# Moving operands of gate and up kept in DRAM as single values and split in place when loaded, the first pair of gate and up interleaved, and the first buffers of the way down moved

## The chip, the cores and the metric

The kernel runs on one core of a Trainium2 chip. The metric is the device time of one execution in microseconds (us). TensorE (PE) does the matrix products, VectorE (DVE) and ScalarE (ACT) the elementwise work, GpSimd (POOL) some elementwise work and the DMAs of one queue, SyncE (SP) issues the DMAs of the other.

## The reference, cut to what matters

One layer of a hybrid decoder: 2048 prompt tokens and 8 sample tokens, D_MODEL = 1024, D_FF = 2816.

```python
# n = RMSNorm(x); one projection of n, split among attention heads and gated linear attention (GLA)
# A = sliding-window attention with sinks, B = chunked GLA
# h = x + W_o [A | B]
# y = h + SwiGLU(RMSNorm(h)):  (silu(z @ w_gate) * (z @ w_up)) @ w_down,  z = RMSNorm(h)
```

All products are wanted to float32 accuracy.

## The kernel before, in words

The program runs through five stages, one after the other: attention (0 to about 380 us of the span), GLA (to 739), W_o with the second RMSNorm (to about 950), gate and up (959 to 1847), down (1853 to 2307). The order on each engine is fixed at build time by a scheduler that lists the instructions by a timeline of its own; engines run their lists in order and wait for each other by semaphores. Buffers lie in pools stacked in SBUF, so a pool of a later stage lies over buffers of an earlier one, and its first write waits for their last use.

**Split values.** A float32 operand is split into a high part (ACT, `split`, L92: a cast to the reduced type) and a low part (DVE or POOL, L93: value minus high part). A product is three matmuls (`mm3`, L104 to L106): high x high, high x low, low x high.

**W_o stage.** Token tiles of 128 run in the order 0, 4, 1, 5, 2, 6, 3, 7, then 8, 12, 9, ... , 15, then the decode tile (8 sample tokens, `ti == NB`). For each, `load_tile` loads the mixed heads (`mr`) and splits them into `mt`; `product` multiplies by W_o (`WO`, two halves of D, L104 to L106; the decode tile's product is L1019), adds h, and writes h to DRAM (L1022); `normalise` makes z (L1030 to L1032), transposes it (L1037, `ps_zT`) and puts it into four tiles `b`. When two tiles j = 0, 1 of one `mt` are there, `operands` forms the seven moving operands of Strassen's method (P1 to P7) from the quarters `b` by four subtractions `t`, **splits each one** into `zhl` (a ring of three buffers in the pool `hlp`) and writes high and low part to DRAM (`zc_d`, L1057, on POOL's queue). The last `mt` is 132 wide, since it takes the decode tokens with it, so its operands wait for the decode tile. `PRODS` is the order P1, P6, P2, P7, P5, P4, P3.

**Gate and up.** The tokens fall into two halves, sb = 0 (512 columns) and sb = 1 (516). At the start of a half the seven split operands `z` are loaded from `zc_d` on SP's queue (L1242, 2 MB each). Then 11 pairs of feed-forward blocks (`fp`) run. For each the weights of gate and of up are loaded (`wrg`, L1179) and turned into seven units each (`units`, `whl`, a ring of 7 buffers, which `dm` of the next stage shares): a sum or difference (L958, L961) and a split. A unit times its z is a product of 4 x 3 matmuls of 512 columns (2 x 12 of 258 at sb = 1). `Strassen.ready` takes the results from PSUM: P1 by ACT (L1149, `gp` for gate and `up` for up), the others by DVE; silu is ACT (L1191), the multiplication L1199. The combined results are written for the way down (`md_d`, L1236, POOL's queue), and the decode columns are kept in `mdec` by ACT (L1227).

**Down.** Four groups of pairs (3, 3, 3 and 2). A group loads W_down (`wrd`), makes seven split units per pair (`dhl`, 22 buffers), and for each of 8 token tiles loads `mr` from `md_d` (L1310), splits its seven parts into `dm`, and multiplies; `decode` does the sample tokens with `mhl`, the split of `mdec`. In SBUF the two `mr` buffers lie over the last z operands used (those of P4 and P3), the first `dhl` buffers over the z of P1, which is free earliest.

## Time and profile before

| | before |
|---|---|
| median of 3 runs | 2312.25 us (2310.04 to 2315.82) |
| profiled execution, and its span | 2311.51 us, 2309.7 us |
| mean granted clock of TensorE | 0.983 |
| PE busy | 2227.1 us, 96% of the span |
| DVE busy | 1600.5 us, 69% |
| ACT busy | 957.2 us, 41% |
| POOL busy | 623.8 us, 27% |
| moved by DMA | 364.57 MB, 158 GB/s on average |

The times of rows below are in us from the span's start; the profiled execution takes 1.8 us more than its span. A row of a timeline gives start, duration, engine (SPq is SP's DMA queue), line, operation, out<-in, and in brackets the idle time before it and what ended that. In a row of windows stand the length, the busy time of PE, PEld (weight loads), DVE, ACT and POOL with their instruction counts, the granted TensorE clock, the DMA share and GB/s. Matmuls are pipelined: what counts is the distance between two starts, not the duration shown.

### The profile page before, as it was taken

To read this page: it belongs to the slowest core of one execution; us is meant where nothing else is said; L and a number is where in the kernel's file an instruction comes from. 1 tells how busy PE (TensorE), PEld (TensorE's weight loads), DVE (VectorE), ACT (ScalarE), POOL (GpSimd) and SP (SyncE) were. 2 spreads that over 40 slices of the span, in tenths; PEclk is the share of its full clock that TensorE was granted. 3 is DMA by queue.
4 is the path that set the end of the run, shared out by engine and by line. 5 is a ranking of instruction groups with operands and counts; after the bars stand their busy time and mean duration, and the time that the engine had idled before them with its cause. 6 is when DMAs were issued, how large, how long until landed. Compare 5 with 4: busy or idle time off the path is not lost.

```text
span 2309.7 us, 34809 instructions
## 1 busy us (share of the span) xinstructions
PE 2227.1 (96%) x12649; PEld 1923.6 (83%) x12649; DVE 1600.5 (69%) x3236; ACT 957.2 (41%) x2120; POOL 623.8 (27%) x791
## 2 busy tenths in 40 slices
PE   8999998999999999699999999999999989999998
PEld 6888886788887788578888889999999968787887
DVE  6787887587776567556666666767676674847477
ACT  5676777343443234323232333333333243535342
POOL 2443434365465133201111110101010122222222
PEclk9999998999998999899999999999999999999999
DMA  7323234245325689872324257323233277878877
GB/s 239 122 75 115 93 108 153 90 157 165 126 87 214 225 275 288 276 247 87 119 79 127 78 177 290 110 84 115 87 111 97 83 225 171 210 165 213 185 184 263
DMA packets 204935, 364.57 MB, mean 158 GB/s; under 512 B 15411, under 2 KB 128332, under 8 KB 200780
## 3 DMA queue, kind: packets, MB, share of 16 engines
q1 hardware_dynamic: 167740, 258.80, 34.2%
q0 software_dynamic: 37024, 103.55, 17.9%
q8 instruction: 100, 1.64, 0.3%
q14 instruction: 71, 0.58, 0.1%
HBM read 211.09 MB, written 152.27 MB: 157 GB/s over the span
## 4 chain that ended last, share of the span: by engine, by line
PE 31%; issue 20%; POOL 5%; DMA 1%; DVE 0%; POOLq 0%; ACT 0%; SPq 0%; DVEq 0%; ACTq 0%
PE ps_b L105 4%; PE ps_b L104 4%; PE ps_b L106 4%; POOL h_d L1329 4%; PE ps_c L105 3%; PE ps_c L104 3%; PE ps_c L106 3%; PE ps_a L105 3%; PE ps_a L106 3%; PE ps_a L104 3%; POOL out_y_prompt_dram L1324 1%; DMA z<-zc_d_P 1%; POOL md_d L1236 1%; DMA zc_d_P<-zhl 0%; DMA wrg<-in_w_gate_dram 0%
## 5 line engine op out<-in xcount | busy, mean ns | idle before, releaser
L104 PE MATMUL ps_b<-z,whl 128*128 128x258 f32 (+1 forms) x792 | 253.8, 321 | 3.2 <-DMA z<-zc_d_P 3.2
L105 PE MATMUL ps_b<-z,whl 128*128 128x258 f32 (+1 forms) x792 | 254.0, 321 | 0.0
L106 PE MATMUL ps_b<-z,whl 128*128 128x258 f32 (+1 forms) x792 | 252.8, 319 | 0.0
L92 ACT CAST dm<-mr 128x384 fp32r<-128x384 f32 (+1 forms) x224 | 108.0, 488 | 188.4 <-PE ps_b L106 97.6
L104 PE MATMUL ps_a<-z,whl 128*128 128x258 f32 (+1 forms) x528 | 170.9, 324 | 8.3 <-DMA z<-zc_d_P 8.3
L105 PE MATMUL ps_a<-z,whl 128*128 128x258 f32 (+1 forms) x528 | 170.7, 323 | 0.0
L106 PE MATMUL ps_a<-z,whl 128*128 128x258 f32 (+1 forms) x528 | 170.3, 323 | 0.0
L104 PE MATMUL ps_c<-z,whl 128*128 128x258 f32 (+1 forms) x528 | 168.6, 319 | 0.9 <-DMA z<-zc_d_P 0.9
L105 PE MATMUL ps_c<-z,whl 128*128 128x258 f32 (+1 forms) x528 | 169.1, 320 | 0.0
L106 PE MATMUL ps_c<-z,whl 128*128 128x258 f32 (+1 forms) x528 | 168.9, 320 | 0.0
L104 PEld LDWEIGHTS ps_b<-z,whl 128*128 128x128 f32 x792 | 149.3, 189 | 15.9 <-DMA z<-zc_d_P 3.5
L106 PEld LDWEIGHTS ps_b<-z,whl 128*128 128x128 f32 x792 | 149.2, 188 | 12.1
L105 PEld LDWEIGHTS ps_b<-z,whl 128*128 128x128 f32 x792 | 149.2, 188 | 11.9
L93 DVE TENSOR_TENSOR dm<-mr,dm 128x384 fp32r<-128x384 f32 (+1 forms) x224 | 114.9, 519 | 59.4 <-ACT dm L92 59.4
L92 ACT CAST whl<-wrg 128x512 fp32r<-128x512 f32 x132 | 81.6, 620 | 150.5 <-PE ps_b L106 81.2
L802 POOL TENSOR_TENSOR bd<-E,qTb 64x128 f32<-64x128 f32 x224 | 127.1, 567 | 60.6 <-ACT E L787 47.2
L93 DVE TENSOR_TENSOR whl<-wrg,whl 128x512 fp32r<-128x512 f32 x132 | 90.9, 688 | 42.9 <-ACT whl L92 42.7
L961 DVE TENSOR_TENSOR gu<-ps_c,gu 128x512 f32<-128x512 f32 (+1 forms) x130 | 77.9, 600 | 61.0 <-PE ps_c L106 60.3
L1236 POOL DMA_DIRECT2D md_d<-m x22 | 15.7, 713 | 373.7 <-DVE m L1199 360.3
L104 PEld LDWEIGHTS ps_a<-z,whl 128*128 128x128 f32 x528 | 100.8, 191 | 17.0 <-issue 4.4
L104 PEld LDWEIGHTS ps_c<-z,whl 128*128 128x128 f32 x528 | 99.8, 189 | 9.3 <-ACT whl L92 1.3
L105 PEld LDWEIGHTS ps_a<-z,whl 128*128 128x128 f32 x528 | 100.5, 190 | 8.2
(385 smaller groups left out, 6625.9 us busy)
## 6 DMA issues: line engine op xcount, KB each, us to landing
mr<-md_d SPq DMA_DIRECT2D x24, 1344.0 KB
zc_d_P<-zhl POOLq DMA_DIRECT2D x49, 512.0 KB, 6.1
wrg<-in_w_gate_dram SPq DMA_DIRECT2D x44, 512.0 KB
wrg<-in_w_up_dram SPq DMA_DIRECT2D x44, 512.0 KB
nT_d<-nT SPq DMA_DIRECT2D x16, 1024.0 KB
zT<-nT_d SPq DMA_DIRECT2D x8, 2048.0 KB
z<-zc_d_P SPq DMA_DIRECT2D x7, 2064.0 KB
z<-zc_d_P SPq DMA_DIRECT2D x7, 2048.0 KB
```

Of the source, the lines that this page charges most:

```text
L92: nc.scalar.copy(h, src)
L93: (eng or nc.vector).tensor_tensor(l, src, h.bitcast(F32), ALU.subtract)
L104: nc.tensor.matmul(ps, lh, rh, start=start, stop=False, skip_group_check=more)
L105: nc.tensor.matmul(ps, lh, rl, start=False, stop=False, skip_group_check=more)
L106: nc.tensor.matmul(ps, ll, rh, start=False, stop=stop, skip_group_check=more)
L802: nc.gpsimd.tensor_tensor(bv[rows, :, h], eo, qo, ALU.mult)
L961: nc.vector.tensor_tensor(out, a, b, ALU.add)
L1236: nc.gpsimd.dma_start(md_d[sb][g][:, :, q, fp - GROUPS[g][0], :], src.rearrange("p (m t) -> p m t", m=4))
L1324: nc.gpsimd.dma_start(O["y_prompt"][0, ti * P:(ti + 1) * P, cols], hq[which])
L1329: nc.gpsimd.dma_start(h_d[ti][:, cols], c, accum_op=ALU.add)
```

## The change

Six edits go together.

- `zc_d` holds single values: `operands` writes `b` and `t` themselves, without the split and the ring `zhl`, half the bytes.
- Each z lies in a pool of its own. It is loaded into the low half of its tile and split there (`split_z`): the high part by ACT, two casts of 128 x 1024, the low part over the loaded value by DVE (P1, P2, P7) or POOL (P6, P5, P4, P3), two subtractions of 128 x 1024 each.
- The pools of W_o are cut so that the z of P1 lies over the two `mt` buffers alone, those of P6 and P2 over the first half of W_o and those of P7 and P5 over the second. The first two `mr` of that stage get buffers of their own. The write of the decode tile's h goes to POOL's queue.
- In the first pair of sb = 0 gate and up alternate in a fixed order, the splits of z are put behind named instructions (`issue_after`), P2's behind gate's copy of P1, and the weights of later pairs are loaded after the last z.
- The copies into `mdec` go from ACT to POOL.
- Down: the two `mr` buffers lie over the z of P1 and P6, the first six `dhl` over P6 and P2, the others below. In the first group pair 0's units come first, then those of pairs 1 and 2 in turn, and the low parts of pairs 0 and 2 are made by POOL.

```diff
-    zc_d = [[dram.tile([P, 2, KD // 2, WIDTHS[sb]], F32, name=f"zc_d{sb}_{q}") for q in PRODS] for sb in range(2)]
+    zc_d = [[dram.tile([P, KD // 2, WIDTHS[sb]], F32, name=f"zc_d{sb}_{q}") for q in PRODS] for sb in range(2)]
...
-        wop = pool(ph, "m_wo", 1, side="right")
-        hlp = pool(ph, "m_hl", 3, side="right")
+        wop = [pool(ph, f"m_wo{dh}", 1, side="right") for dh in range(2)]
+        mrp = pool(ph, "m_mr", 2, side="right")
...
-                mr = hlp.tile([P, 1056], F32, tag="hl", name="mr")[:, :1024]
+                mr = mrp.tile([P, 1024], F32, tag="mr", name="mr")
...
-            nc.sync.dma_start(h_d[ti] if ti < NB else hdec_d, h[:n])
+            (nc.sync if ti < NB else nc.gpsimd).dma_start(h_d[ti] if ti < NB else hdec_d, h[:n])
...
             for q, src in enumerate((b11, t2, b21, t3, t1, t4, b22)):
-                hl = hlp.tile([P, 2, 4, 132], F32R, tag="hl", name="zhl")
-                split(hl[:, 0, :, :w], hl[:, 1, :, :w], src)
-                nc.gpsimd.dma_start(zc_d[sb][q][:, :, :, mt * P:mt * P + w], hl[:, :, :, :w].bitcast(F32))
+                nc.gpsimd.dma_start(zc_d[sb][q][:, :, mt * P:mt * P + w], src)
...
-        zcp = pool(ph, "g_zc", 1, side="right")
+        zcp = {name: pool(ph, f"g_z{q}", 1, side="right") for q, name in enumerate(PRODS)}
...
-        def pair(sb, fp, zc):
+        def split_z(z, name, behind=()):
+            with ExitStack() as es:
+                for ins in behind:
+                    es.enter_context(tc.issue_after(ins.ins))
+                for ks in (slice(0, 2), slice(2, 4)):
+                    split(z[:, 0, ks], z[:, 1, ks], z[:, 1, ks].bitcast(F32), None if name in ("P1", "P2", "P7") else nc.gpsimd)
+        def pair(sb, fp, zc, ug, uu):
...
-            ug, uu = load_w(w_g, fp), load_w(w_u, fp)
+                return mm.ins
             if len(pieces) == 1:
+                last = None
                 for q in PRODS:
-                    prod(sg, q, next(ug))
-                    prod(su, q, next(uu))
+                    for st, us in ((sg, ug), (su, uu)):
+                        with tc.issue_after(last) if fp == 0 and last else nullcontext():
+                            with tc.issue_after(begun.pop().ins) if begun and fp == 1 else nullcontext():
+                                hl = next(us)
+                            last = prod(st, q, hl)
+                        if fp == 0:
+                            for name, *behind in {("P1", sg): (("P2", sg.kept),), ("P1", su): (("P7", su.kept),),
+                                                 ("P2", sg): (("P5", sg.silu),), ("P7", su): (("P4", sg.silu, su.mark),),
+                                                 ("P5", sg): (("P3", sg.silu),)}.get((q, st), ()):
+                                split_z(zc[name], name, behind)
+                if fp == 0:
+                    begun.extend([su.mark] * 4)
...
-                    nc.scalar.copy(mdec[:, 2 * fp + f, 4 * j:4 * j + 4], m[:, 512:516])
+                    nc.gpsimd.tensor_copy(mdec[:, 2 * fp + f, 4 * j:4 * j + 4], m[:, 512:516])
...
-            zc = {name: zcp.tile([P, 2, 4, 516], F32R, tag=f"z{q}", name=f"z{q}")[:, :, :, :WIDTHS[sb]]
-                  for q, name in reversed(list(enumerate(PRODS)))}
+            zc = {name: zcp[name].tile([P, 2, 4, 516], F32R, tag=f"z{q}", name=f"z{q}")[:, :, :, :WIDTHS[sb]]
+                  for q, name in enumerate(PRODS)}
+            raws = load_w(w_g, 0), load_w(w_u, 0)
             for q, name in enumerate(PRODS):
-                nc.sync.dma_start(zc[name].bitcast(F32), zc_d[sb][q])
+                come = nc.sync.dma_start(zc[name][:, 1].bitcast(F32), zc_d[sb][q])
+            for name in PRODS[:2] if sb == 0 else PRODS:
+                split_z(zc[name], name)
             for fp in range(NP):
-                pair(sb, fp, zc)
+                pair(sb, fp, zc, *raws)
+                if fp + 1 < NP:
+                    with tc.issue_after(come.ins):
+                        raws = load_w(w_g, fp + 1), load_w(w_u, fp + 1)
...
-        wdp = pool(ph, "d_w", 22, side="right")
-        mrp = pool(ph, "d_mr", 2, side="right")
+        mrps = [pool(ph, f"d_mr{i}", 1, side="right") for i in range(2)]
+        wdps = [pool(ph, f"d_w{i}", n, side="right") for i, n in enumerate((6, 8, 8))]
+        made = [0]
+        def unit_tile():
+            j = made[0] % 22
+            made[0] += 1
+            return wdps[(j >= 6) + (j >= 14)].tile([P, 2, 512], F32R, tag="w", name="dhl")
...
-                uq = {}
-                b = (r0[:, 0:512], r0[:, 512:], r1[:, 0:512], r1[:, 512:])
-                for q, src in zip(PRODS, sums_b(*b)):
-                    hl = wdp.tile([P, 2, 512], F32R, tag="w", name="dhl")
-                    split(hl[:, 0], hl[:, 1], src)
-                    uq[q] = hl
-                us.append(uq)
+                for q, src in zip(PRODS, sums_b(r0[:, 0:512], r0[:, 512:], r1[:, 0:512], r1[:, 512:])):
+                    hl = unit_tile()
+                    split(hl[:, 0], hl[:, 1], src, nc.gpsimd if p in (0, 2) else None)
+                    us[p - p0][q] = hl
+                    yield
+            for some in ([[p0], [p0 + 1, p0 + 2]] if g == 0 else [[p] for p in range(p0, p1)]):
+                for _ in zip(*[pair_units(p) for p in some]):
...
-                mr = mrp.tile([P, 7, 384], F32, tag="mr", name="mr")[:, :, :npr * P]
+                mr = mrps[mi % 2].tile([P, 7, 384], F32, tag="mr", name="mr")[:, :, :npr * P]
```

`issue_after(x)` makes the scheduler list what stands under it behind x; it adds no wait on the chip.

On SP's queue the first load of z (P1's) now stands ahead of the last prompt tile's write of h, and no write of the decode tile's h stands in front of the others; before, all seven stood behind it. On PE, at the end of W_o, before (z_10184 is P1's z):

```order
L1019 MATMUL ps_wo<-WO_8479,mixdec 40x512 x16
L1019 MATMUL ps_wo<-WO_8480,mixdec 40x512 x16
L1037 MATMUL ps_zT<-ident,z 128x128 x8
L1037 MATMUL ps_zT<-ident,z 128x8 x8
L104 MATMUL ps_a<-z_10184,whl 128x512
```

Now the transposes of the decode tile (`128x8`) stand behind the products P1 and P6 of gate and of up, 48 matmuls later (z_10033 is P6's z, z_10034 P2's):

```order
L105 MATMUL ps_b<-z_10033,whl 128x512
L106 MATMUL ps_b<-z_10033,whl 128x512
L1038 MATMUL ps_zT<-ident,z 128x8 x8
L104 MATMUL ps_a<-z_10034,whl 128x512
L105 MATMUL ps_a<-z_10034,whl 128x512
```

The decode tile, and with it the last operands of sb = 1, comes two products later on PE; P2 follows it.

ACT at the same place. Before, its last operand splits stand ahead of the copies of gate's and up's P1:

```order
L1030 ACTIVATE z,ss<-h 8x1024
L92 CAST zhl<-b_9842 128x528
L92 CAST zhl<-t_10119 128x528
L92 CAST zhl<-b_9843 128x528
L92 CAST zhl<-t_10120 128x528
L92 CAST zhl<-t_10118 128x528
L92 CAST zhl<-t_10121 128x528
L92 CAST zhl<-b_9845 128x528
L1149 COPY gp_10193<-ps_a 128x512
```

Now (z_10032 is P1's, z_10035 P7's):

```order
L92 CAST z_10032<-z_10032 128x2x512 x2
L92 CAST z_10033<-z_10033 128x2x512 x2
L1041 COPY b_9722<-ps_zT 128x4x128
L1031 ACTIVATE z,ss<-h 8x1024
L92 CAST whl<-sx 128x512 x3
L92 CAST whl<-wrg 128x512
L1150 COPY gp_10063<-ps_a 128x512
L92 CAST z_10034<-z_10034 128x2x512 x2
L1150 COPY up_10066<-ps_a 128x512
L92 CAST z_10035<-z_10035 128x2x512 x2
```

The seven `zhl` casts are gone; the casts of P2's z stand directly behind gate's copy `gp`. That copy is written into a buffer that lies over `t0`, one of the subtraction tiles of `operands`, so it waits for the write of the last `t0` to `zc_d`.

POOL around the start of the way down. Before:

```order
L1236 DMA md_d_3_4861<-gu_17470 512x1x128
L1236 DMA md_d_3_4861<-m_17940 512x1x128
L1236 DMA md_d_3_4861<-gu_17943 512x1x128
L1236 DMA md_d_3_4861<-gp_17941 512x1x128
L1258 MEMSET mhl 128x880
L1236 DMA md_d_3_4861<-up_17944 512x1x128
L1236 DMA md_d_3_4861<-uu_17946 512x1x128
```

Now:

```order
L1258 DMA md_d_3_4861<-m_17858 512x1x128
L93 TENSOR_TENSOR dhl<-wrd,dhl 128x512
L93 TENSOR_TENSOR dhl<-ty,dhl 128x512
L93 TENSOR_TENSOR dhl<-wrd,dhl 128x512
L93 TENSOR_TENSOR dhl<-tx,dhl 128x512
L93 TENSOR_TENSOR dhl<-wrd,dhl 128x512
L1249 COPY mdec<-gu_17861 128x4
L1258 DMA md_d_3_4861<-gu_17861 512x1x128
L93 TENSOR_TENSOR dhl<-tx,dhl 128x512
L93 TENSOR_TENSOR dhl<-ty,dhl 128x512
L1249 COPY mdec<-gp_17859 128x4
L1258 DMA md_d_3_4861<-gp_17859 512x1x128
```

The seven low parts of pair 0 stand between the last writes of `md_d`; seven more, of pair 2, follow behind the memset of `mhl`.

More of the change, by code (lines that the diff above doesn't have):

```diff
@@ L1 @@
 import math
-from contextlib import ExitStack
+from contextlib import ExitStack, nullcontext
 import numpy as np
@@ L105, in mm3 @@
         nc.tensor.matmul(ps, lh, rl, start=False, stop=False, skip_group_check=more)
-        nc.tensor.matmul(ps, ll, rh, start=False, stop=stop, skip_group_check=more)
+        return nc.tensor.matmul(ps, ll, rh, start=False, stop=stop, skip_group_check=more)
     def rstd(ss, n, scale, cols=1):
@@ L975, in hymba_kernel @@
         acc = pool(ph, "m_acc", 4, space=PSUM)
-        WO = [wop.tile([P, 2, KD, 512], F32R, name=f"WO{dh}") for dh in range(2)]
+        WO = [wop[dh].tile([P, 2, KD, 512], F32R, name=f"WO{dh}") for dh in range(2)]
         gBf = zp.tile([P, D], F32, name="gBf", bufs=1)
@@ L1148, in ready @@
             if q == "P1":
-                nc.scalar.copy(p1, ps)
+                self.kept = nc.scalar.copy(p1, ps)
             elif q == "P6":
@@ L1190, in gate_done @@
                 out = m11[:, c0:c1] if which == "11" else c
-                nc.scalar.activation(out, c, AF.Silu)
+                sg.silu = nc.scalar.activation(out, c, AF.Silu)
             sg = Strassen(Ps(), W, pieces, "g", gate_done)
@@ L1264, in group, with pair_units @@
             last = g == len(GROUPS) - 1
-            us = []
-            for p in range(p0, p1):
+            us = [{} for p in range(p0, p1)]
+            def pair_units(p):
                 raws = []
```

13 lines of the change are left out of this document (8 added, 5 removed).

## The prediction

> **What bounds the kernel now.** First the busy shares of the page, then windows of 50 us, to see where PE pauses.
>
> ```profile
> PE 2227.1 (96%) x12649; PEld 1923.6 (83%) x12649; DVE 1600.5 (69%) x3236; ACT 957.2 (41%) x2120; POOL 623.8 (27%) x791
> ...
> 850.00:900.00 50.00, 50.00 (x238) 41.66 (x238) 33.78 (x51) 19.43 (x32) 14.86 (x19) 1.00 0.92 292
> 900.00:950.00 50.00, 46.93 (x227) 36.67 (x225) 38.56 (x61) 19.80 (x34) 14.74 (x18) 1.00 0.84 252
> 950.00:1000.00 50.00, 33.69 (x120) 25.96 (x121) 19.01 (x33) 12.87 (x21) 7.25 (x9) 0.80 1.00 341
> 1000.00:1050.00 50.00, 50.00 (x217) 40.46 (x216) 34.95 (x56) 15.89 (x27) 6.43 (x9) 1.00 0.46 153
> 1400.00:1450.00 50.00, 50.00 (x404) 49.34 (x403) 35.48 (x68) 16.88 (x37) 7.92 (x11) 1.00 0.66 244
> 1800.00:1850.00 50.00, 47.02 (x393) 46.81 (x391) 31.68 (x64) 14.27 (x34) 7.82 (x11) 0.99 0.32 102
> 1850.00:1900.00 50.00, 43.26 (x169) 30.61 (x170) 40.42 (x71) 23.38 (x47) 10.00 (x13) 0.91 0.71 218
> 1900.00:1950.00 50.00, 50.00 (x222) 41.44 (x221) 23.38 (x42) 15.79 (x32) 11.88 (x14) 1.00 0.81 184
> ```
>
> PE is the bound: 96% busy, and in the middle of W_o (850), of gate and up (1000, 1400) and of down (1900) it never pauses. So what the change takes from ACT, DVE and DMA inside these stages is worth nothing there. There are two holes that it touches: 900 to 1000, where DMA stands at 1.00, and 1800 to 1900. The waits of PE in these two places:
>
> ```profile
> PE ps_a L104 <- DMA z<-zc_d_P: 8.3, 2, 4.3
> PE ps_zT L1037 <- DVE z L1032: 6.9, 1, 6.9
> PE ps_b L104 <- DMA z<-zc_d_P: 3.2, 2, 3.0
> PE ps_c L104 <- DMA z<-zc_d_P: 0.9, 1, 0.9
> ...
> PE ps_a L104 <- ACT dm L92: 6.5, 1, 6.5
> PE ps_c L104 <- ACT dhl L92: 2.2, 1, 2.2
> ```
>
> The first four sum to 19.3 us at the start of gate and up, on the loads of z and the decode tile's transposes. The last two, and under 1 us of small ones, are the 2.98 + 6.74 = 9.7 us at the start of down. After a wait PE also runs slower for a while:
>
> ```profile
> 945.90 1.03 PE L1037 MATMUL ps_zT<-ident,z 128*128 128x128 f32 x8
> 953.83 0.99 PE L1037 MATMUL ps_zT<-ident,z 8*128 8x8 f32 x8 [6.90 <-DVE z L1032]
> 959.10 0.80 PE L104 MATMUL ps_a<-z,whl 128*128 128x512 f32 x1 [4.28 <-DMA z<-zc_d_P]
> 959.69 0.63 PE L105 MATMUL ps_a<-z,whl 128*128 128x512 f32 x1
> 960.12 0.63 PE L106 MATMUL ps_a<-z,whl 128*128 128x512 f32 x1
> ...
> 990.14 0.39 PE L106 MATMUL ps_b<-z,whl 128*128 128x512 f32 x1
> 990.37 0.39 PE L104 MATMUL ps_b<-z,whl 128*128 128x512 f32 x1
> ```
>
> Starts are 0.43 us apart after the wait and 0.23 later, 0.20 lost per matmul. By the window at 950 (clock 0.80), 112 matmuls at 50/217 = 0.23 and the 1 us of transposes should fill 26.8 us and fill 33.7: 6 to 7 us lost, call it 6. So this hole costs 19.3 + 6 = 25.3 us. In the same way 169 matmuls at 50/222 would fill 38.1 us of the window at 1850 and fill 43.3; as records can be missing I take 4, and 9.7 + 4 = 13.7 us for the second hole.
>
> **Start of gate and up.** What runs there:
>
> ```profile
> 950.34 0.29 SPq L1022 DMA_DIRECT2D hdec_d<-h  x1
> 950.81 40.70 SPq L1242 DMA_DIRECT2D z<-zc_d_P  x7
> ...
> 975.25 0.58 ACT L1149 COPY gp<-ps_a 128x512 f32<-128x512 f32 x1
> ...
> zc_d_P<-zhl POOLq DMA_DIRECT2D x7, 528.0 KB, 9.4
> ...
> md_d<-gu POOLq DMA_DIRECT2D x4, 256.0 KB, 4.3
> ...
> L92 ACT CAST mt<-mr 128x1024 fp32r<-128x1024 f32 x16 | 16.8, 1047 | 31.5 <-PE ps_wo L106 29.3 <-DMA mr<-mix_d 2.2
> L93 DVE TENSOR_TENSOR mt<-mr,mt 128x1024 fp32r<-128x1024 f32 x16 | 20.4, 1277 | 1.8 <-ACT mt L92 1.7
> L836 POOL TENSOR_TENSOR kd<-kd,kTb 128x512 f32<-128x512 f32 x8 | 10.2, 1280 | 12.5 <-ACT kd L835 6.5 <-issue 5.4 <-POOL bd L802 0.5
> L1057 POOL DMA_DIRECT2D zc_d_P<-zhl x56 | 48.3, 873 | 101.9 <-DVE zhl L93 90.1 <-DVE rs_v L111 11.6
> ```
>
> Seven loads of 2 MB queue behind the decode tile's write at 950.34 and take 40.7 us. The first took 8.3 us to P1 (950.81 to 959.10), of which 2.1 MB at 341 GB/s are 6.2; 1 MB would take 3.1 + 2.1 = 5.2 us. Now the walk in the new order. P1's buffer is free at W_o's last prompt matmul, about 937.6 (eight transposes and 32 decode matmuls of 0.23 lie between it and 945.90), so z lands at 942.8. Two casts of 1.05 and two subtractions of 1.28 on DVE end at 946.4, before tile 15's transposes end at 946.9: P1 waits for nothing and 24 matmuls take 5.6 us, to 952.5. P6's z waits for the first half of the decode product (942.2) and lands at 947.4; a POOL subtraction of 128 x 1024 is not in the trace, and at twice L836 takes 2.56 us. The two halves are ready at 951.0 and, behind the issue of hdec_d's write, 954.4: half a microsecond of wait, P6 ends at 958.6, the decode transposes at 959.6.
>
> Then comes a wait of its own. POOL issues the seven last writes of zc_d, 0.87 each: t0's, the fourth, leaves at 963.1 and t1's at 964.8. A write of 256 KB lands in 4.3. So ACT's gp copy (0.58), which lies over t0, ends at 968.0, the first cast of P2's z at 969.0; DVE's addition for P6, which waits for t1's write, ends about 969.8, and the first subtraction of P2 at 971.1. PE stands from 959.6 to about 971: 11.3 us, and some 14 matmuls at half speed, 2.8. The loads of P7 to P3 are in long before, but their splits now share DVE and POOL with the weight units. POOL needs 6 x 2.56 = 15.4 us for P5, P4 and P3 while about 12 two-operand DVE instructions stand beside it. How these two get along is shown by
>
> ```profile
> 352.35 1.89 POOL L372 TENSOR_TENSOR S<-S,den 128x1024 f32<-128x1024 f32 x1
> ...
> 353.15 1.64 DVE L93 TENSOR_TENSOR WQ<-wrq,WQ 128x512 fp32r<-128x512 f32 x1 [0.82 <-ACT WQ L92]
> 355.20 0.68 DVE L93 TENSOR_TENSOR WQ<-wrq,WQ 128x512 fp32r<-128x512 f32 x1
> ```
>
> The same DVE subtraction takes 0.68 alone and 1.64 where it starts under a POOL instruction: it ends 0.55 after POOL does (354.24). So DVE's subtractions partly wait. Pair 1's first units come about 2 us late for it. Loss now 0.5 + 11.3 + 2.8 + 2.2 = 16.8 against 25.3: **-8.5 us**. Bounds: if the writes land at once after their issue and nothing stretches, 6.5 less again (-15); if they take the 9.4 us of the 528 KB rows, 5.1 more, and the stretching 2 more (-1.4).
>
> [...]
>
> **The half switch (1400).** 14 casts, 6 DVE and 8 POOL subtractions are new. P3's z, the last, is needed 6 products after the new half starts. A product is 24 matmuls at 50/404, 2.97 us, so there are 17.8 us, and its load, casts and POOL halves need 5.2 + 2.1 + 5.1 = 12.4. DVE is busy 35.5 of 50 there. With 7.7 of its own and all 20.5 of POOL's it would be 13.7 us late per 50, which a lead of seven units (7 x 2.97 = 20.8) covers. Hidden then, with DVE behind; I take **+1.5**, ends 0 and +6.
>
> **Start of down.**
>
> ```profile
> 1847.05 0.80 SPq L1310 DMA_DIRECT2D mr<-md_d  x2
> ...
> 1852.95 2.99 ACT L92 CAST dm<-mr 128x384 fp32r<-128x384 f32 x7 [4.36 <-DMA mr<-md_d]
> ...
> 1853.52 0.80 PE L104 MATMUL ps_a<-dhl,dm 128*128 128x512 f32 x1 [6.50 <-ACT dm L92]
> ...
> L93 DVE TENSOR_TENSOR dhl<-wrd,dhl 128x512 fp32r<-128x512 f32 x33 | 22.0, 685 | 0.0
> L93 DVE TENSOR_TENSOR dm<-mr,dm 128x384 fp32r<-128x384 f32 x168 | 91.7, 552 | 54.2 <-ACT dm L92 54.2
> ```
>
> mr waits for the last product, since it lies under its z, and 5.9 us later dm begins. Now it lies over P1's and P6's z: free after up's P1, six products of 2.97 before the end (1829.2), landed by 1835, split before 1847. That wait goes. Late next are DVE's units. Between POOL's first low part (about 1837, up's P2 being done and its cast made) and the split of mhl, which the decode product waits for, stand 9 POOL low parts, 9 x 1.28 = 11.5 us, and on DVE 10 instructions of 0.69, 5 of 0.55, 6 half-width ones of about 0.35 and small ones, 12.3 us, with 6 reads of PSUM, 2.4. Side by side, DVE is through shortly after its last inputs, about 1854, where PE wants mhl at 1851 to 1852: some 3 us of waits in pieces, and 1 of slow clock, 9.7 less than now. One after the other they end at 1837 + 26.2 = 1863: 11.5 us of wait with the same 4 of slow clock, 1.8 more than now. The row at 353.15 is nearer to the second, but POOL stands still between (for writes of md_d and for casts), and then DVE runs on: **-3**, ends -9.7 and +1.8.
>
> **The rest.** Tile 4's mt is split before the stage begins, and a wait for it goes:
>
> ```profile
> 757.15 0.50 PE L106 MATMUL ps_wo<-WO,mt 128*128 128x512 f32 x1 [1.14 <-DVE mt L93]
> ```
>
> against it stands a split of 1.28 on DVE earlier, among GLA's last steps: **-0.5**, ends -1.1 and +2. 56 splits of zhl fall away in W_o, some 35 us of ACT and 38 of DVE, and half of zc_d's bytes: nothing, PE covers them (50.00 of 50). 44 small copies into mdec move to POOL, 27% busy: nothing, short of the last pair's, which stand among the low parts above. The order of the weights' loads after the last z only delays pair 1, whose units wait for the z splits anyway: nothing.
>
> **Sum.** -8.5 + 1.5 - 3 - 0.5 = -10.5. The profiled execution took 2311.5 (span 2309.7 and 1.8 around it), so 2301.0; it lies 0.7 below the median of 2312.25: **2301.7 us**.
>
> **Rivals.**
> 1. POOL and DVE exclude each other throughout. Gate and up then gain 8.5 - 2.2 = 6.3, the switch costs 4, down 1.8, and the W_o stage is as above: 2312.2 - 1.0 = 2311.2. For it: the row at 353.15. Against: POOL is idle for much of these stretches.
> 2. They hardly meet. Gate and up gain 11, down 9.7, the switch costs nothing: 2312.2 - 21.2 = 2291. For it: POOL's 27%; against: the same row.
> 3. Slower: POOL's in-place subtractions become what PE waits for, in the first pair and at the switch. Each half takes 2.56 us plus waits for DVE. In the first pair a product of gate and of up lasts 5.6 us, so with halves of h us three tiles are late by 2h - 5.6 each; at the switch four tiles lose 2h - 5.1 each, less the slack of 5.4. At h = 3.9 that is 12 us, as much as the other three terms gain, and from there on it decides; at 5 it is 27: 2312.2 - 12 + 27 = 2327. Against: DVE's instructions there are short (0.69).
> 4. The wait before P2 eats the gain: the writes of zc_d at the 9.4 us row. 2301.7 + 5.1 = 2306.8.
>
> **Chances.** The forecast 0.48 (its own range 2296 to 2307), rival 1 0.18, rival 2 0.18, rival 3 0.07, rival 4 0.09. A measurement tells about 0.3%, 7 us, from no change: under 2305.3 fall 0.42 of the forecast's, all of rival 2 and a third of rival 4, above 2319.2 most of rival 3: faster 0.63, same 0.32, slower 0.05. The range goes from 2289, just past rival 2, to 2313, past rival 1; some 0.15 is left out.
>
> **What would show it.** In the changed profile P1 starts within 2 us of tile 15's transposes; PE waits 9 to 13 us before P2 on ACT or DVE behind writes of zc_d; no wait over 2 us at 1400; the first dm product of down starts within 5 us of the last gate and up matmul; DVE rows of 0.69 stretch to 1 to 2 us beside POOL's. I am wrong if P2's wait is under 5 or over 16 us, if POOL's halves take over 3.5 us, or if PE idles at 1400.

## The result: slower by 0.6%, and the profile after

| | before | after |
|---|---|---|
| median of 6 runs | 2313.55 us (2310.04 to 2316.23) | 2327.6 us (2323.99 to 2334.19) |
| ratio, 95% interval | | 1.0063 [1.0044, 1.0081] |
| profiled execution, span, clock | 2311.51 us, 2309.7 us, 0.983 | 2334.19 us, 2332.4 us, 0.978 |

The forecast was 2301.7 us (2289 to 2313), faster: wrong in sign. The profiled execution of after is the slowest of its six runs, 6.6 us over their median, so sums below go by stages. The first line is from the page of after, the others are windows of 50 us, to lay beside those of before.

```profile
PE 2237.2 (96%) x12649; PEld 1930.6 (83%) x12649; DVE 1606.5 (69%) x3178; ACT 942.1 (40%) x2048; POOL 693.9 (30%) x866
```

```profile
950.00:1000.00 50.00, 33.98 (x147) 25.55 (x145) 29.30 (x33) 21.20 (x28) 21.67 (x16) 0.86 0.70 226
1000.00:1050.00 50.00, 49.71 (x215) 39.95 (x214) 41.66 (x61) 17.17 (x29) 11.58 (x11) 1.00 0.28 85
1400.00:1450.00 50.00, 43.70 (x313) 42.39 (x312) 42.85 (x58) 18.64 (x35) 21.16 (x15) 0.90 0.37 117
...
1850.00:1900.00 50.00, 38.93 (x183) 29.73 (x183) 46.06 (x62) 19.55 (x39) 28.62 (x29) 0.90 0.49 146
```

The busy share of DVE is the same 69% as before, and nothing in the page's first lines tells why the kernel is slower. The windows do. At 950 PE now starts 147 matmuls where it started 120. At 1400, where it never paused before (404 matmuls), it starts 313 at a clock of 0.90; 91 are missing, and at 50/404 = 0.124 us each that is 11.3 us: 6.3 in which PE stands, and some 5 because the 313 would fill 38.8 us at that pace and take 43.7. The hole at 1850 is deeper (38.93 busy for 43.26). What PE waits for in these three places:

```profile
PE ps_a L104 <- ACT z L92: 9.4, 1, 9.4
PE ps_a L105 <- DVE z L93: 3.6, 1, 3.6
PE ps_b L105 <- POOL z L93: 3.0, 2, 1.7
...
PE ps_a L104 <- ACT gp L1150: 3.3, 1, 3.3
PE ps_b L104 <- DVE gu L961: 3.0, 2, 2.2
...
PE ps_b L105 <- DVE dhl L93: 4.8, 1, 4.8
PE ps_a L104 <- DVE uu L961: 3.0, 1, 3.0
PE ps_ea L1329 <- DVE mhl L93: 2.6, 1, 2.6
```

The first three are at the start of gate and up, the next two at the half switch, the last three at the start of down. Of 32.7 us only 3.0 are waits for POOL's low parts. The rest of the last two groups, 16.7 us, are waits for DVE, or for an ACT copy that stands behind something of DVE's.

Cut at four marks of PE (first W_o matmul, tile 15's transposes, first matmul of the second half, last gate and up matmul, last matmul), the traces of all kernels of this study give these lengths in us. "Before" stands twice, since it was profiled a second time with the last experiments.

| kernel | W_o | first half | second half | down | last matmul to end |
|---|---|---|---|---|---|
| before | 206.8, 207.6 | 457.6, 457.1 | 443.3, 443.3 | 455.8, 456.7 | 7.2, 7.2 |
| after | 209.3 | 450.0 | 455.5 | 463.5 | 10.5 |
| z_dve | 209.6 | 445.3 | 444.2 | 458.5 | 10.0 |
| down_dve | 209.5 | 449.3 | 454.7 | 453.1 | 10.0 |
| all_dve | 209.4 | 444.9 | 443.9 | 455.4 | 10.0 |
| down_old | 209.2 | 449.9 | 454.7 | 453.5 | 10.0 |
| all_olddown | 211.0 | 444.2 | 443.4 | 454.9 | 10.0 |
| p2_free | 210.9 | 439.0 | 443.3 | 457.4 | 10.0 |
| wo_late | 211.8 | 445.3 | 443.4 | 454.0 | 10.1 |
| pool_idle | 210.5 | 444.2 | 447.8 | 453.8 | 10.0 |
| idle_long | 209.4 | 449.4 | 458.0 | 458.3 | 10.3 |
| idle_copy | 211.1 | 444.3 | 444.6 | 453.5 | 10.0 |
| pool_short | 210.6 | 454.9 | 454.3 | 463.5 | 10.0 |

So the change wins 7.6 us in the first half and loses 12.2 in the second, 7.7 in down, 2.5 in W_o and 3.3 at the end. The beginning of W_o moves by several us from kernel to kernel (736.3 to 744.0) and is left out of this. Down is not sharp either: the seven kernels that have the new down with no low parts on POOL lie between 453.1 and 458.3.

**What happens at the half switch**, from the timeline of after:

```profile
1401.21 5.87 POOL L93 TENSOR_TENSOR z<-z 128x1032 fp32r<-128x1032 f32 x2
1401.29 0.68 DVE L93 TENSOR_TENSOR whl<-wrg,whl 128x512 fp32r<-128x512 f32 x1
1401.89 0.68 DVE L961 TENSOR_TENSOR gp<-ps_b,gp 128x512 f32<-128x512 f32 x1
1402.49 2.31 DVE L93 TENSOR_TENSOR whl<-sx,whl 128x512 fp32r<-128x512 f32 x1
...
1405.33 2.30 DVE L961 TENSOR_TENSOR sx<-wrg 128x512 f32<-128x512 f32 x1
...
1407.74 0.62 ACT L92 CAST whl<-sx 128x512 fp32r<-128x512 f32 x1 [4.50 <-DVE sx L961]
...
1411.82 0.64 ACT L1150 COPY gp<-ps_a 128x258 f32<-128x258 f32 x2
...
1412.23 0.39 PE L104 MATMUL ps_a<-z,whl 128*128 128x258 f32 x1 [3.26 <-ACT gp L1150]
```

POOL makes two low parts. A DVE addition that reads PSUM (1401.89) takes its 0.68 us beside them; two DVE instructions with both operands in SBUF take 2.31 and 2.30 for 0.68. ACT stands 4.50 us for `sx`; its cast of `sx` starts at 1407.74, and the copy `gp`, which empties the PSUM bank that PE wants next, stands six instructions further down its list and starts at 1411.82. PE waits 3.26 us for it. No z was late: the weight units had their lead of seven, but the results stand in two or three PSUM banks of each kind, a far shorter lead, and these are emptied by the same two queues. At the start of down it is starker:

```profile
1848.00 1.37 POOL L93 TENSOR_TENSOR dhl<-wrd,dhl 128x512 fp32r<-128x512 f32 x1
...
1849.25 1.35 POOL L93 TENSOR_TENSOR dhl<-ty,dhl 128x512 fp32r<-128x512 f32 x1
1849.71 5.54 DVE L93 TENSOR_TENSOR dm<-mr,dm 128x384 fp32r<-128x384 f32 x2
1850.50 1.35 POOL L93 TENSOR_TENSOR dhl<-wrd,dhl 128x512 fp32r<-128x512 f32 x1
1851.74 1.35 POOL L93 TENSOR_TENSOR dhl<-tx,dhl 128x512 fp32r<-128x512 f32 x1
...
1852.99 1.35 POOL L93 TENSOR_TENSOR dhl<-wrd,dhl 128x512 fp32r<-128x512 f32 x1
```

Five POOL subtractions run back to back. Two DVE subtractions of 0.55 us each take 5.54 together and end just behind the train. Here DVE does not get in between two of POOL's instructions. It is not always so: in the timeline above `whl<-sx` of 1402.49 ends at 1404.80, 2.3 us ahead of the end of POOL's two (1407.08), so DVE came in behind the first. From 945 us on, in the trace of after, 19 of DVE's two-operand rows are stretched beside POOL's subtractions: 16 end behind the one subtraction then running, as a rule 0.55 us later, and three are held through two, two and four. None of the 11 DVE rows there that read PSUM is stretched.

### The profile page after: what moved, and what is told of

The parts are those of the page before. It is cut to its first block, busy times and chain, and to the rows that moved or that the text cites. A ratio compares the mean times of both kernels' runs of the same rounds, so it can differ in the third digit from the quotient of the medians.

```text
span 2332.4 us, 34723 instructions
## 1 busy us (share of the span) xinstructions
PE 2237.2 (96%) x12649; PEld 1930.6 (83%) x12649; DVE 1606.5 (69%) x3178; ACT 942.1 (40%) x2048; POOL 693.9 (30%) x866
## 4 chain that ended last, share of the span: by engine, by line
PE 79%; DVE 6%; issue 5%; DMA 4%; POOL 3%; ACT 2%; SPq 0%; POOLq 0%; DVEq 0%; ACTq 0%
PE ps_b L105 7%; PE ps_b L104 7%; PE ps_b L106 7%; PE ps_a L105 5%; PE ps_a L106 5%; PE ps_a L104 5%; PE ps_c L105 5%; PE ps_c L106 4%; PE ps_c L104 4%; PE ps_d L104 3%; PE ps_d L106 3%; PE ps_d L105 3%; PE ps_wo L104 3%; PE ps_wo L105 3%; PE ps_wo L106 3%
## 5 line engine op out<-in xcount | busy, mean ns | idle before, releaser
L104 PE MATMUL ps_a<-z,whl 128*128 128x258 f32 (+1 forms) x528 | 170.5, 323 | 12.7 <-ACT z L92 9.4
L93 DVE TENSOR_TENSOR dm<-mr,dm 128x384 fp32r<-128x384 f32 (+1 forms) x224 | 120.5, 541 | 63.3 <-ACT dm L92 63.0
L961 DVE TENSOR_TENSOR gu<-ps_b,gp 128x512 f32<-128x512 f32 (+1 forms) x130 | 77.5, 597 | 48.0 <-PE ps_b L106 39.3
L92 ACT CAST whl<-sy 128x512 fp32r<-128x512 f32 x88 | 54.4, 619 | 137.0 <-PE ps_b L106 79.8
```

Source lines behind the costliest of these rows:

```text
L92: nc.scalar.copy(h, src)
L93: (eng or nc.vector).tensor_tensor(l, src, h.bitcast(F32), ALU.subtract)
L104: nc.tensor.matmul(ps, lh, rh, start=start, stop=False, skip_group_check=more)
L961: return nc.vector.tensor_tensor(out, a, b, ALU.add)
```

## The experiments

### Who makes the low parts

Theory L: POOL's subtractions hold DVE's instructions with two SBUF operands; I took it that a train of them holds DVE for the whole train. Theory Q: the many subtractions are a burden whoever makes them. Four kernels, timed in 5 rounds each beside before.

z_dve, all low parts of z on DVE:

```diff
-split(z[:, 0, ks], z[:, 1, ks], z[:, 1, ks].bitcast(F32), None if name in ("P1", "P2", "P7") else nc.gpsimd)
+split(z[:, 0, ks], z[:, 1, ks], z[:, 1, ks].bitcast(F32), None)
```

> The changed kernel with all low parts of z made by DVE; POOL makes none of them. Theory L (a train of POOL subtractions shuts out DVE's instructions with two SBUF operands): the rows of 2.2 to 4.1 us on DVE around 1386 to 1423 go back to 0.7, the switch to sb = 1 costs 0 to 3 us instead of 12, and the decode tile's chain, no longer behind POOL's halves, brings P2 2 to 4 us earlier: 2327.6 - 9 - 3 = about 2315 (2310 to 2319). Rival Q (the splits of z simply stand in order ahead of the evacuations of PSUM, whoever makes them): DVE has 8 x 1.2 us more to do at the switch, PE waits as long or longer: 2326 to 2336.

down_dve, all low parts of down on DVE:

```diff
-split(hl[:, 0], hl[:, 1], src, nc.gpsimd if p in (0, 2) else None)
+split(hl[:, 0], hl[:, 1], src, None)
```

> The changed kernel with the low parts of pairs 0 and 2 of the first group of down made by DVE. Theory L: DVE's row of 5.5 us at 1849.7 falls to 1.0, the waits on DVE uu, dhl and mhl (3.0, 4.8, 2.6 us) shrink to 3 us in all: 2327.6 - 8 = 2319 (2315 to 2323). Rival Q (DVE has too much to do there in any case): 9.7 us of low parts move back to DVE, the first dm product comes no earlier: 2326 to 2334.

all_dve, both edits:

> Both edits: no subtraction of the change is on POOL. Theory L: both gains, 2327.6 - 12 - 8 = 2307 (2302 to 2312), so faster than the kernel before by 2 to 11 us. Rival Q: 2325 to 2337.

down_old, the changed kernel with the down stage of before:

```diff
-mrps = [pool(ph, f"d_mr{i}", 1, side="right") for i in range(2)]
-wdps = [pool(ph, f"d_w{i}", n, side="right") for i, n in enumerate((6, 8, 8))]
+wdp = pool(ph, "d_w", 22, side="right")
+mrp = pool(ph, "d_mr", 2, side="right")
...
-split(hl[:, 0], hl[:, 1], src, nc.gpsimd if p in (0, 2) else None)
+split(hl[:, 0], hl[:, 1], src)
```

> The changed kernel with the whole stage of down as it was (one pool of 22 units and one of two mr buffers, pairs in order, low parts on DVE); the copies into mdec stay on POOL. Theory L: down takes 456 us from the last gate and up matmul to the last matmul, as before, instead of 463: 2327.6 - 7.5 = 2320 (2317 to 2323). Rival: down is longer for a reason that lies ahead of it (the buffers under it, late writes of md_d): 2326 to 2330.

| | median, us | ratio to before, 95% |
|---|---|---|
| z_dve | 2311.52 | 0.9995 [0.9985, 1.0006] |
| down_dve | 2317.07 | 1.0015 [1.0005, 1.0025] |
| all_dve | 2304.63 | 0.9968 [0.9956, 0.998] |
| down_old | 2319.19 | 1.0022 [1.0012, 1.0033] |

All came out as L had it; they tell who must not make the low parts, but not whether the hold lasts for one instruction or for a train. With every low part back on DVE the same change is faster than before, by 0.2 to 0.44%. The second half falls from 455.5 to 443.9 us, though DVE does 8 more subtractions of 1.22 us there. DVE's groups between 1380 and 1470, first of after, then of all_dve (count, then busy time and mean ns):

```profile
L93 DVE TENSOR_TENSOR whl<-sy,whl 128x512 fp32r<-128x512 f32 x9 | 8.6, 954 | 0.7 <-ACT whl L92 0.7
...
L958 DVE TENSOR_TENSOR sx<-wrg 128x512 f32<-128x512 f32 x4 | 6.2, 1541 | 5.6 <-DMA wrg<-in_w_up_dram 4.5 <-DMA wrg<-in_w_gate_dram 1.0
...
L958 DVE TENSOR_TENSOR gu<-gp,uu 128x512 f32<-128x512 f32 x2 | 3.8, 1900 | 0.0
```

```profile
L93 DVE TENSOR_TENSOR z<-z 128x1032 fp32r<-128x1032 f32 x12 | 14.6, 1222 | 1.6 <-ACT z L92 1.6
...
L93 DVE TENSOR_TENSOR whl<-sy,whl 128x512 fp32r<-128x512 f32 x11 | 7.5, 684 | 0.6 <-ACT whl L92 0.6
...
L958 DVE TENSOR_TENSOR sx<-wrg 128x512 f32<-128x512 f32 x5 | 3.4, 689 | 4.2 <-DMA wrg<-in_w_up_dram 3.1 <-DMA wrg<-in_w_gate_dram 1.1
```

Forms of 0.68 us stretch to 0.95, 1.54 and 1.90 in after and keep 0.68 in all_dve.

### Is it the hold, or are POOL's low parts simply late?

z_dve takes away both. Three kernels keep all_dve's program and let POOL do extra work behind the casts of z for P6, P5, P4 and P3 that **nobody reads**: nothing can be late for it. In the traces of pool_idle and idle_long PE, DVE and ACT have the same instructions in the same order as in all_dve; only POOL's differ (in idle_copy two of DVE's have changed places as well). A fourth keeps POOL's low parts and cuts them small.

pool_idle, eight subtractions of 128 x 256 per z:

```diff
+for k in range(ks.start, ks.stop):
+    for c in (0, 256):
+        hi = z[:, 0, k, c:c + 256].bitcast(F32)
+        nc.gpsimd.tensor_tensor(idle, hi, hi, ALU.subtract)
```

> The changed kernel with all low parts on DVE; in addition POOL makes, behind each pair of casts of the z of P6, P5, P4 and P3 in both halves, four subtractions of 128 x 256 of the cast tile with itself into a spare buffer that nobody reads (16 KB a time, eight per z tile, about as long as the low parts it made in the changed kernel). No engine waits for these. Theory L, POOL's instructions with two SBUF operands hold DVE's, whoever wants their result: DVE's subtractions beside them stretch from 0.69 to 2 to 5 us, the second half of gate and up takes 448 to 456 us and not 443.9, time 2312 to 2322. Rival R, the third of the prediction, it was the late low parts themselves that PE waited for: second half 443 to 445 us, time 2303 to 2307.

idle_long, four subtractions of 128 x 512 per z, between two rows:

```diff
+for k in (0, 1):
+    a, b = (z[:, 0, ks.start + i].bitcast(F32) for i in (k, 1 - k))
+    nc.gpsimd.tensor_tensor(idle[:, :W], a, b, ALU.subtract)
```

> The changed kernel with all low parts on DVE; POOL makes behind each pair of casts of the z of P6, P5, P4 and P3 two subtractions of 128 x 512 (516 in the second half) between two cast rows into a spare bf16 buffer that nobody reads, four per z tile, about as much time as its low parts took in the change. Theory A: these are twice as long as the pieces of 256, so DVE's rows beside them stretch more than there (0.77 to 0.80 for 0.68), and the second half of gate and up takes 448 to 452 us (447.8 with the short ones), time 2308 to 2314. Rival R, what PE waited for in the change was the low parts themselves: 443 to 445 us, time 2303 to 2307.

idle_copy, eight copies of 128 x 512 per z (one SBUF operand):

```diff
+for k in (0, 1, 0, 1):
+    nc.gpsimd.tensor_copy(idle[:, :W], z[:, 0, ks.start + k].bitcast(F32))
```

> The same as the kernel with idle subtractions of 512, but POOL makes four copies of a cast row (one SBUF operand in place of two) into the spare buffer behind each pair of casts. If only POOL's instructions with two SBUF operands hold DVE's, DVE's rows stay at 0.68 to 0.70 beside the copies, the second half of gate and up takes 443 to 445 us, time 2303 to 2307. If any POOL work in SBUF holds them, the rows stretch as beside the subtractions and the second half takes 447 us or more, time 2308 to 2314.

pool_short, the changed kernel with POOL's low parts in eight pieces per z:

```diff
-split(z[:, 0, ks], z[:, 1, ks], z[:, 1, ks].bitcast(F32), nc.gpsimd)
+nc.scalar.copy(z[:, 0, ks], z[:, 1, ks].bitcast(F32))
+for k in range(ks.start, ks.stop):
+    for c in (slice(0, 256), slice(256, z.shape[-1])):
+        l = z[:, 1, k, c]
+        nc.gpsimd.tensor_tensor(l, l.bitcast(F32), z[:, 0, k, c].bitcast(F32), ALU.subtract)
```

> The changed kernel with POOL's low parts of z cut into pieces of 128 x 256 (and the rest of the row), eight to a tile instead of two; casts, buffers and down as in the change. Theory A, a waiting engine gets in between two instructions of the other, so what DVE loses grows with the length of one POOL instruction: at the half switch DVE's rows of 128 x 512 stay near 0.7 to 0.9 us (in the changed kernel 0.95 to 1.9 on average), POOL's pieces stretch instead, the second half of gate and up takes 444 to 449 us in place of 455.5, and the time is 2315 to 2322. Theory T, POOL keeps the access for its whole queued train however it is cut: DVE's rows stretch as before, second half 453 to 457, time 2325 to 2331.

| 3 rounds each | median, us | ratio to before, 95% | second half, us |
|---|---|---|---|
| pool_idle | 2310.68 | 0.999 [0.9978, 1.0001] | 447.8 |
| idle_long | 2326.65 | 1.0058 [1.0042, 1.0073] | 458.0 |
| idle_copy | 2306.89 | 0.9976 [0.9964, 0.9988] | 444.6 |
| pool_short | 2331.79 | 1.0088 [1.0068, 1.0109] | 454.3 |

**idle_long** settles it: POOL work that nobody waits for costs 22 us over all_dve's 2304.63, more than I expected of either theory, and more than the low parts of z themselves (down_dve has them on POOL and lies 12.4 above all_dve). Of the 9.6 us between those two 5.2 stand in down, where they are the longest and the shortest of the seven kernels named above; why the rest is more is open. PE's waits at its half switch, then POOL's and DVE's groups of 1380 to 1470:

```profile
PE ps_b L104 <- DVE gu L961: 4.3, 1, 4.3
PE ps_c L104 <- ACT whl L92: 2.0, 1, 2.0
PE ps_c L106 <- DVE whl L93: 1.9, 1, 1.9
PE ps_a L104 <- ACT gp L1150: 1.3, 1, 1.3
```

```profile
L1196 POOL TENSOR_TENSOR idle<-z 128x516 bf16<-128x516 f32 x16 | 28.4, 1778 | 1.0
```

```profile
L93 DVE TENSOR_TENSOR z<-z 128x1032 fp32r<-128x1032 f32 x12 | 20.1, 1682 | 0.0
```

The waits are of the same kind as in after, and DVE's subtractions take 1.68 for 1.22 us. Late low parts on POOL are not needed for the loss at the switch. How much longer DVE's subtractions and additions take than their usual lengths, from 25 us ahead of the half switch to 65 behind it, lies beside the second half like this:

| us | all_dve | idle_copy | pool_idle | idle_long | after | down_dve | pool_short |
|---|---|---|---|---|---|---|---|
| DVE held | 0.1 | 6.0 | 7.2 | 14.4 | 15.8 | 15.8 | 16.0 |
| second half | 443.9 | 444.6 | 447.8 | 458.0 | 455.5 | 454.7 | 454.3 |

Six us are nearly covered, 14 to 16 are not. In idle_long no train is needed either: POOL's pieces stand 0.08 us apart, and all of the 28 stretched DVE rows end behind the one piece then running.

**pool_short** was to decide how the hold ends: whether DVE gets in where POOL's instructions are short. From its timeline, two trains of eight pieces:

```profile
1383.60 5.66 POOL L1198 TENSOR_TENSOR z<-z 128x256 fp32r<-128x256 f32 x8
1385.04 4.78 DVE L958 TENSOR_TENSOR sx<-wrg 128x512 f32<-128x512 f32 x1 [2.46 <-DMA wrg<-in_w_up_dram]
...
1400.24 10.31 POOL L1198 TENSOR_TENSOR z<-z 128x256 fp32r<-128x256 f32 x8
1407.69 1.11 DVE L961 TENSOR_TENSOR up<-gu,gu 128x512 f32<-128x512 f32 x1
1408.72 1.23 DVE L958 TENSOR_TENSOR uu<-m,gu 128x512 f32<-128x512 f32 x1
```

Beside the first train, eight pieces of 0.71 us, one DVE addition of 0.69 is held for 4.78, to 0.56 us behind their end. Beside the second, DVE gets in after every piece, and POOL, held in its turn, takes 10.31 for its eight. Both happen: of 32 stretched DVE rows 26 end behind one piece, five are held through three to eight. So neither theory holds throughout, and what decides between the two cases is open. Cutting the low parts up did not help the time, which is at the edge of what I had put on theory T (2325 to 2331 expected, 2331.79 measured); that it came near it does not bear T out.

**idle_copy** keeps POOL busy for longer than idle_long does, 67 us of copies for 55 of subtractions (each count has in it the time in which POOL itself was held: the copies took 0.97 to 1.13 us on average and the subtractions 1.66 to 1.78), and its time is all_dve's within the interval. So a longer list on POOL's queue is not what costs. I had expected DVE's rows to be left alone beside one-operand work, and they were not quite; its z rows take 1.37 us:

```profile
L1195 POOL CAST idle<-z 128x516 bf16<-128x516 f32 x30 | 34.8, 1158 | 1.3
```

```profile
L93 DVE TENSOR_TENSOR z<-z 128x1032 fp32r<-128x1032 f32 x11 | 15.1, 1369 | 0.0
```

**pool_idle** alone would have been inconclusive: 2310.68 lies between the two expectations. There it is POOL that was held, eight pieces in 16.02 us (8.29 for the eight before), and DVE's z rows take 1.37 as beside copies:

```profile
1392.64 16.02 POOL L1197 TENSOR_TENSOR idle<-z 128x256 f32<-128x256 f32 x8
```

Its pieces are as short as pool_short's, but both their operands are the same row, and all go to one buffer and stand 0.08 us apart: all of the 35 stretched DVE rows end behind one piece. They have half the length of idle_long's and hold DVE half as long (7.2 us for 14.4). So where DVE gets in after every piece, short pieces may well be worth it; the operands were not the same, so this is not shown.

### What the new down is worth

all_olddown is all_dve with the whole down stage of before (the edits of z_dve and down_old together), 5 rounds.

> The changed kernel with all low parts of z on DVE and the whole down stage as it was before the change (its pools, its order of units, its splits). Theory G, the earlier start of down is given back inside the stage: the first product of down comes 6.5 to 7.5 us behind the last gate and up matmul, yet down as a whole (last gate and up matmul to last matmul) takes 453 to 456 us, as with the new down on DVE (455.4), and the time is 2304.6 give or take 2 (2302.5 to 2307). Rival K, the new down is worth its 5 us: down takes 459 to 461 us and the time is 2308 to 2312.

2304.03 us, 0.9962 [0.9948, 0.9975], down 454.9 us: theory G, by the time above all, since down varies by more than the two differ. The first product of down comes 1.8 us behind the last of gate and up in all_dve and 7.4 in all_olddown, and that is given back inside the stage. In all_dve PE waits there for

```profile
PE ps_b L104 <- ACT dhl L92: 4.0, 1, 4.0
PE ps_a L104 <- ACT dhl L92: 2.6, 1, 2.6
```

that is, for units, 4.0 us at the second product and 2.6 at 2098.7, two groups on; all_olddown has 1.3 for the first kind and none of the second.

### The wait before P2

In after ACT's copy of P1's product stands 7.71 us for a write of `t` to DRAM, and the casts of P2's z behind it:

```profile
977.18 0.58 ACT L1150 COPY gp<-ps_a 128x512 f32<-128x512 f32 x1 [7.71 <-DMA zc_d_P<-t]
977.66 1.99 ACT L92 CAST z<-z 128x1024 fp32r<-128x1024 f32 x2
```

p2_free is all_dve with other buffers under `gp`: those `b` of even tiles, whose writes are long done.

```diff
-bp = pool(ph, "m_b", 1, side="right")
-tp = pool(ph, "m_t", 1, side="right")
+bodd, tp = (pool(ph, n, 1, side="right") for n in ("m_b1", "m_t"))
+beven = pool(ph, "m_b0", 1, side="right")
...
-bs[...] = [bp.tile([P, 4, 132], F32, tag=f"b{q}", name=f"b{q}", bufs=2) for q in range(4)]
+bs[...] = [(bodd if ti % 2 else beven).tile([P, 4, 132], F32, tag=f"b{q}", name=f"b{q}") for q in range(4)]
```

> The changed kernel with all low parts on DVE, and in W_o the buffers of the block tiles b laid out so that the even set, free early, lies under the gate partials gp and u2 of the first pair, where t0 to t2 lay; nothing else moves in the order of W_o. Theory W, the copy of P1's product waits for the last writes of t0 (6.0 us on ACT) and so PE before P2 (8.3 and 2.3 us): both waits fall to under 3 us together, the stretch from tile 15's transposes to the half switch falls from 444.9 to 436 to 440 us, and the time is 2295 to 2300. Rival V, P2's splits are late for the decode tile and the weight units on ACT and DVE anyway: PE still waits 6 us or more there and the time is 2302 to 2307.

2300.19 us in 5 rounds, 0.9935 [0.9919, 0.9952], the fastest kernel of the study. The first half falls to 439.0 us, theory W, and PE's two waits go from 8.3 and 2.3 us in all_dve to

```profile
964.91 0.49 PE L104 MATMUL ps_a<-z,whl 128*128 128x512 f32 x1 [2.19 <-ACT z L92]
967.22 0.62 PE L105 MATMUL ps_a<-z,whl 128*128 128x512 f32 x1 [1.81 <-DVE z L93]
```

4.0 together, where I expected under 3; three products on a wait of 1.7 us for the copy `up` comes new.

### W_o, and before once more

wo_late is all_dve with the low parts of the first two mix tiles held back to where they stood before:

```diff
+with tc.issue_after(late[tiles.index(ti)].ins) if ti in tiles[:2] else nullcontext():
     split(mt[:, 0], mt[:, 1], mr)
```

(`late` holds the last masked copy into AT, one of GLA's tiles, and GLA's last state update.)

> The changed kernel with all low parts on DVE, and the low parts of the first two mix tiles held on DVE behind the last masked copy into AT and the last state update, which is where they stood before the change. Theory E, the two early splits delay GLA's last masked copies and the start of W_o costs 2.5 us for it: PE's wait on AT goes from 3.8 to under 3, W_o from its first matmul to tile 15's transposes takes 206.5 to 207.5 us and not 209.3, time 2301 to 2303.5. Rival N, the 2.5 us have another cause, or the waits for mt that come back (3.0 and 1.2 us before the change) cost as much: 209 us and 2303.5 to 2307.

2307.32 us in 5 rounds, 0.9979 [0.9968, 0.999], and W_o is not shorter but 211.8 us: theory E falls, and it is worse than its rival had it too (209 us, 2303.5 to 2307). PE's wait on AT goes to 1.9 as expected, and waits on the held splits come instead:

```profile
PE ps_wo L108 <- DVE mt L95: 3.4, 1, 3.4
...
PE ps_wo L106 <- ACT mt L94: 2.5, 1, 2.5
```

before_again is before itself, one profile, 2312.23 us:

> The kernel before, unchanged, profiled once more to see how far its stages vary between executions. The kernels with the change show the first W_o matmul at 736 to 744 us with the same program ahead of it, W_o itself from there to tile 15's transposes 209.2 to 211.8 us (before: 206.8) and 10.0 to 10.4 us from the last matmul to the end (before: 7.2). If these are variation, this profile shows W_o at 208 to 211 us and an end of 8 to 10; if they belong to the change, 206.5 to 207.2 and 7.0 to 7.4. Time 2307 to 2318 either way.

Its W_o takes 207.6 us and its end 7.2. So both belong to the change: 209.2 to 211.8 us for W_o and 10.0 to 10.5 for the end stand in all twelve kernels that have it.

In W_o PE stands less than before (4.5 us for 5.3). What is longer is the matmuls behind its one long wait:

```profile
775.80 1.94 PE L1038 MATMUL ps_zT<-ident,z 128*128 128x128 f32 x8 [3.77 <-DVE z L1033]
779.08 0.63 PE L105 MATMUL ps_wo<-WO,mt 128*128 128x512 f32 x1
779.51 0.63 PE L104 MATMUL ps_wo<-WO,mt 128*128 128x512 f32 x1
```

From 774.5 the granted clock is 0.50 for 6.8 us, and starts are 0.43 apart for 0.23; before has 1.00 from 745 to 950. That is some 3 us, less the 0.8 of waits saved, about the 2.5.

## Why the prediction was wrong, step by step

| step | predicted | measured, after | all_dve |
|---|---|---|---|
| start of gate and up | -8.5 | -7.6 | -12.7 |
| half switch | +1.5 | +12.2 | +0.6 |
| down | -3 | +7.7 | -0.4 |
| W_o | -0.5 | +2.5 | +2.6 |
| end | none | +3.3 | +2.8 |

**Right: the start of gate and up.** P1 starts 0.8 us behind the start of tile 15's transposes and waits for nothing. PE then waits 9.4 + 3.6 = 13.0 us before P2 (11.3 forecast), behind the writes of `zc_d` that I had named; p2_free shows this mechanism by taking it away. P6's POOL halves take 2.35 and 2.38 us (2.56 forecast) and cost 3.0 us of waits for 0.5. Too small was the price of POOL's low parts: without them the step is worth 12.7, so they cost 5.1 us here, where 2.7 stood.

**Wrong: the half switch, the step that failed first.** The step read "it would be 13.7 us late per 50, which a lead of seven units (7 x 2.97 = 20.8) covers". The lead exists, and no unit's z was late. But DVE and ACT also empty the PSUM banks from the same queues, and those have far less: PE waited 6.3 us for `gp` and `gu`, and some 5 more went at a granted clock of 0.90 for these 50 us, for which the step had no term. DVE's burden was not put too low: I had laid POOL's 20.5 us on it, and DVE was held for 15.8. The cover was the wrong one. "No wait over 2 us at 1400" names the same mistake: there were 3.3 and 2.2.

**Wrong: the start of down.** The first product of down came closer as forecast, 3.2 us behind the last of gate and up for 6.8. "Side by side" did not come: the step took the row at 353.15, a DVE instruction held to POOL's end, as a hold in part, since "POOL stands still between" its instructions. Where POOL's low parts queue, it does not stand still: the five at 1848 take 6.3 us, 1.35 to 1.37 each. PE waited 3.0, 4.8 and 2.6 us, 10.3 in all: near the 11.5 of the bound "one after the other". The stage lost more than that bound's 1.8, in part because another 2.3 us wait for a unit, and a granted clock of 0.79 for the 8 us behind it, come at 2122, far behind the start. Moving these low parts to DVE wins 6.9 us (z_dve to all_dve) or 10.5 (after to down_dve). Even then the term is near zero and not -9.7, the gain bound: "late next are DVE's units" was right, but the 4.0 + 2.6 us on units in all_dve are as much as the wait that went, and the second of them comes at 2098.7, 255 us into the stage, where I did not look.

**Wrong in sign: W_o.** Measured +2.5 for -0.5. The early splits are not its cause (wo_late). In after and all_dve the first z of W_o makes PE wait 3.8 us, where before PE waited 5.3 for `mt`; the granted clock behind that wait, 0.50 for 6.8 us in after, which the sum had at nothing, is what is longer. Why it falls there, and not behind the waits of before, is open. **Missed: the end.** One of POOL's last instructions, a DRAIN, takes 7.13 us in after and 4.32 in before, and this difference of 2.8 is most of the end's 3.3. Before, then after (the last figure ahead of the comma is the longest, in ns):

```profile
L1394 POOLq DRAIN  x3: 40/93/4316, 2304.7 to 2309.5; - x3
L1437 POOLq DRAIN  x3: 40/235/7132, 2324.1 to 2332.2; - x3
```

The end is longer with the old down too (10.0 us in down_old and all_olddown for 7.2). Why is open.

**The rivals.** Rival 1 (POOL and DVE exclude each other throughout) had the mechanism (DVE was held for 15.8 us at the switch), with the switch at 4 and down at 1.8: both a third or less of what was measured. Rival 3 gave the time, 2327, but by another mechanism and so by luck: its halves of h = 5 us took 2.35 to 3.04, and idle_long shows that lateness of POOL's results is not needed. What I gave 0.07 for its condition should have stood on rival 1 with a higher price.

**The hold, as the traces show it.** In after 19 of DVE's rows with two SBUF operands are stretched beside POOL's subtractions, and none of the 11 that read PSUM (0.68 us beside POOL). Most end behind one instruction of POOL's (16 of 19 in after, all 28 in idle_long), but not all: eight queued instructions of 0.71 us held one of DVE's for 4.78 in pool_short. So here a hold did outlast the instruction.

## What to carry to other kernels

Before elementwise work goes to GpSimd, ask what VectorE does beside it. Here, with two SBUF operands on both sides, one engine waited while the other worked, mostly for one instruction (a DVE row of 0.68 us took 2.31) and at times for a train (one of 0.69 took 4.78); cutting the low parts into pieces did not help (2331.79 us for 2327.6), and copies were nearly free (2306.89 us for 2304.63). When a stage "has a lead", check which work has it: here the queues that made operands ahead also emptied the PSUM banks, and the lead there was far shorter, two or three banks for seven units. A wait removed at a stage's start is worth only what the next late thing leaves (in all_dve the first product of down comes 5.6 us closer than in all_olddown, and down takes 455.4 us for 454.9), so follow the stage to its end, and look under every new buffer for the transfer that still holds the old one (7.71 us for `gp` in after).

## What the runs showed of the hardware that I had not expected

- The hold went over instruction ends: 5.54 us for two DVE subtractions of 0.55 beside five POOL subtractions of 1.35; 4.78 for one of 0.69 beside eight of 0.71. Most rows end behind one: 16 of 19 in after, 26 of 32 in pool_short, all in idle_long and pool_idle.
- It went both ways: beside a busy DVE, eight POOL subtractions of 128 x 256 took 16.02 us in pool_idle, and 10.31 in pool_short, where eight others took 5.66.
- 67 us of POOL copies in SBUF beside a busy DVE cost no time that can be measured (0.9976 [0.9964, 0.9988] for 0.9968 [0.9956, 0.998]), though they hold DVE for 6.0 us at the half switch; 55 us of subtractions hold it for 14.4 there and cost 22 us.
- Behind a wait of 3.8 us in W_o the granted clock of TensorE was 0.50 for 6.8 us in after, and starts of matmuls went from 0.23 to 0.43 us apart.
